# The closing tail of a two-layer encoder: a written-down order, split last columns, 1/rms by root and one Newton step

## The chip, the cores and the metric

The kernel runs on one core of one Trainium2 chip. The metric is the device time of one execution in microseconds, of which three were taken: 839.72, 839.94 and 842.06, median 839.94. One execution was recorded by the hardware profiler; its time is 839.72 and its span, from the first to the last instruction, 837.6. TensorE is called PE in the profile's rows, VectorE DVE, ScalarE ACT, GpSimd POOL, SyncE SP (it issues nearly all transfers).

## The reference

Two residual layers over 256 tokens of width 2048, each with a normalisation ahead, and a normalisation at the end. What matters here is the end:

```python
def rms_norm(x, g):
    xf = x.astype(jnp.float32)
    y = xf * lax.rsqrt(jnp.mean(xf * xf, axis=-1, keepdims=True) + EPS)
    return (y * g.astype(jnp.float32)).astype(x.dtype)
...
        if layer % 2 == 0:
            h = h + even_layer(y, w_in_even[i], w_out_even[i], rpb_b[i])
        else:
            h = h + odd_layer(y, w_in_odd[i], w_out_odd[i], sinks_c[i], qnorm_d[i], knorm_d[i])
    return rms_norm(h, final_g)
```

Each layer ends in an output projection, `mix @ w_out`, with a `mix` of 256 x 2048. All is float32 in and out.

## The kernel before

Tokens lie on the 128 partitions in two tiles, t = 0 and 1; the 2048 columns of the residual `h` are four blocks of 512, n = 0 to 3, `h[n][:, t, :]`. In the names of instructions these four are h_91 to h_94. Products in float32 are made of three matmuls (`mm3`, L100) out of operands split in two parts each, hence the three lines L102, L103, L104 in every product.

The output projection of the odd layer runs over eight head pairs. `close_layer` (L588) adds seven of them to `h` block by block; `ahead` loads the weights of the eighth into buffers of their own (named x in the rows) and the final weights `final_g`, spread over the partitions, into `gfin[n]`. `tail_odd` (L700) then does the last pair, and the final normalisation.

For each tile t, and each block n in it:

- `product_out` (L476): six matmuls of 512 columns into one of three buffers of PSUM (`ps_at`, L48). TensorE waits for a buffer until the addition three products earlier has read it.
- `add_h` (L495, VectorE): `h` += product.
- a Square on ScalarE (L722), which writes its result nowhere of use and gives the sum of squares of the block, `ss[n]`, by a read-out that is recorded as an instruction of its own.
- in the first tile, for the blocks 0 to 2, a multiplication of `h` by `gfin` (L724, VectorE).

After the third block the three sums so far are added (`head`, L728 and L729). After the fourth, `rsqrt_column` (L163) computes 1/rms for each row: an integer estimate and three Newton steps, nine instructions of one column on VectorE. `finish` (L704) scales a block by it and issues its output transfer: by one instruction that also multiplies by `gfin` (L707), or, for the blocks weighted already, on VectorE (L709) or ScalarE (L711).

The order of the instructions on each engine is decided by a scheduler that goes by priorities and takes the program's order among equals. Three things steer it here: `tc.high_priority(400)` moves the small operations on columns up, `tc.issue_after` puts one `finish` behind the last Square, and `tc.keep_in_program_order` (used by `pinned`, L85, for loads alone) keeps instructions in the order in which they are written. Every engine works its instructions off in order, and waits at the first one whose operands are not there.

Of the kernel before, what the change touches and what calls it, by code (L numbers as in the profile page):

```python
# [9 lines left out]
F32 = mybir.dt.float32  # L10
# [7 lines left out]
P = 128  # L18
# [16 lines left out]
def encoder(ctx, tc, a, out):  # L35
# [112 lines left out]
    def rsqrt(dst, ss, n, mean):  # L148
# [6 lines left out]
        for it in range(3):  # L155
# [5 lines left out]
            y = z  # L161

    def rsqrt_column(dst, ss, mean, rest):  # L163

        col = lambda name: sm.tile([P, 1], F32, tag="rc_" + name, name="rc_" + name)
        x = col("x")
        nc.vector.tensor_scalar(x, ss, mean, rest, ALU.mult, ALU.add)
        y = sm.tile([P, 1], I32, tag="rc_s", name="rc_s")
        nc.vector.tensor_scalar(y, x.bitcast(I32), -0.5, 1597463007.0, ALU.mult, ALU.add)
        y = y.bitcast(F32)  # L170
        half = col("half")
        nc.vector.tensor_scalar_mul(half, x, -0.5)
        for it in range(3):
            t = col("t")
            nc.vector.tensor_scalar(t, y, y, half, ALU.mult, ALU.mult)
            z = dst if it == 2 else col("z")
            nc.vector.tensor_scalar(z, t, 1.5, y, ALU.add, ALU.mult)
            y = z
# [521 lines left out]
    def tail_odd(order):  # L700

        scale = []

        def finish(n, t):  # L704
            y, r = h[n][:, t, :], scale[t]
            if t == 1 or n == NN - 1:
                nc.vector.scalar_tensor_tensor(y, y, r, gfin[n], ALU.mult, ALU.mult)  # L707
            elif n == 1:
                nc.vector.tensor_scalar_mul(y, y, r)  # L709
            else:  # L710
                nc.scalar.mul(y, y, r)  # L711
            nc.sync.dma_start(out[t * P : (t + 1) * P, n * 512 : (n + 1) * 512], y)

        for t in range(2):
            ss = [sm.tile([P, 1], F32, tag=f"fss{n}", name="fss") for n in range(NN)]
            head = None
            for n in range(NN):
                acc = ps_at.tile([P, 512], F32, tag="at", name="ps_t")
                product_out(acc, final[n], order[0], t, True, True)
                add_h(n, t, acc)  # L720
                junk = tp.tile([P, 512], BF16, tag="junk", name="junk", bufs=1)
                square = nc.scalar.activation(junk, h[n][:, t, :], AF.Square, accum_out=ss[n])  # L722
                if t == 0 and n < NN - 1:
                    nc.vector.tensor_mul(h[n][:, t, :], h[n][:, t, :], gfin[n])  # L724
# [102 lines left out]
```

## Time and profile before

| | |
|---|---|
| device time, three runs | 839.72, 839.94, 842.06 us |
| profiled execution: time, span | 839.72, 837.6 us |
| start of the tail's first matmul | 816.52 us |
| last matmul of the tail starts | 827.17 us |
| last instruction of VectorE starts, lasts | 833.68, 0.75 us |
| output transfers | 8 of 256 KB, issue to landing 2.1 us |
| products, additions, Squares in the tail | 8 x 6 matmuls, 8, 8 |

The page gives each engine's busy time and the chain of work that ended last: followed back from the last instruction, at each step to what released it, or to the instruction before it on its engine. A row of the timeline has the start in us from the span's start, the duration, engine, line, operation, what is written from what, and in brackets the idle time of the engine ahead of it with what ended it. A row of groups has the line, the count behind an x, the busy time in us, the mean duration in ns and the idle time ahead. Matmuls are pipelined: a row of 0.39 us is followed by the next after 0.23.

### The profile page before, as it was taken

How to read it: one execution, taken by the hardware profiler on the slowest of the kernel's cores; microseconds unless marked ns; L12 is line 12 of the kernel's file. 1: busy time of each engine (PE TensorE's matmuls, PEld its weight loads, DVE VectorE, ACT ScalarE, POOL GpSimd, SP SyncE). 2: the span in 40 equal slices, each digit the busy share in tenths (PEclk: the TensorE clock that was granted, in tenths of full speed). 3: DMA queues.
4: the chain of work that ended last, by engine and by line, in shares of the span. 5: the costliest groups of instructions: out<-in, count | busy, mean ns of one | idle time of the engine just before them, and what ended most of it. 6: DMA issues, size and time to landing. Idle time of an engine off the chain costs nothing.

```text
span 837.6 us, 11876 instructions
## 1 busy us (share of the span) xinstructions
PE 821.5 (98%) x4472; PEld 707.2 (84%) x4472; DVE 559.5 (67%) x873; ACT 445.1 (53%) x706; POOL 18.8 (2%) x24
## 2 busy tenths in 40 slices
PE   7999999999999999999999999999999999999995
PEld 5888888888888888888888888888899888888884
DVE  5677575667757675576645787786976666766547
ACT  6755454555445554455443565556666555664433
POOL 0000000000001010010000000000000000000000
PEclk9999999999999999999999999999999999999998
DMA  7976765655566565665555555654545555655622
GB/s 253 374 228 204 236 208 170 209 176 175 178 199 194 171 199 168 201 196 160 172 184 192 176 175 180 193 184 150 165 162 191 182 179 188 194 191 193 226 90 100
DMA packets 55577, 158.51 MB, mean 189 GB/s; under 512 B 14112, under 2 KB 15008, under 8 KB 55456
## 3 DMA queue, kind: packets, MB, share of 16 engines
q1 hardware_dynamic: 55376, 157.74, 57.7%
q8 instruction: 35, 0.57, 0.3%
q14 instruction: 22, 0.18, 0.1%
q10 hardware_dynamic: 144, 0.02, 0.0%
HBM read 155.64 MB, written 3.05 MB: 189 GB/s over the span
## 4 chain that ended last, share of the span: by engine, by line
PE 97%; DVE 1%; DMA 1%; ACT 0%; SPq 0%; issue 0%; DVEq 0%; ACTq 0%
PE ps_f L250 33%; PE ps_f L254 16%; PE ps_t L103 13%; PE ps_t L104 13%; PE ps_t L102 13%; PE ps_pt L439 2%; PE ps_s L103 1%; PE ps_s L104 1%; PE ps_out L103 1%; PE ps_out L104 1%; PE ps_s L102 1%; PE ps_out L102 1%; DMA wraw<-in_even_t 1%; PE ps_ht L610 0%; DVE h L495 0%; PE ps_tr L352 0%
## 5 line engine op out<-in xcount | busy, mean ns | idle before, releaser
L70 DVE TENSOR_TENSOR wlo<-wraw,whi 128x1024 fp32r<-128x1024 f32 (+1 forms) x269 | 329.5, 1225 | 209.7 <-ACT whi L69 208.6
L69 ACT CAST whi<-wraw 128x1024 fp32r<-128x1024 f32 (+1 forms) x269 | 281.8, 1048 | 345.5 <-PE ps_t L104 146.9
L250 PE MATMUL ps_f<-x,whi 128*128 128x512 f32 x1184 | 374.0, 397 | 0.0
L254 PEld LDWEIGHTS ps_f<-x,wlo 128*128 128x128 f32 x1184 | 222.3, 188 | 53.0 <-DVE wlo L70 0.7
L254 PE MATMUL ps_f<-x,wlo 128*128 128x256 f32 x1184 | 233.4, 278 | 0.0
L250 PEld LDWEIGHTS ps_f<-x,whi 128*128 128x128 f32 x1184 | 180.9, 189 | 0.4
L102 PE MATMUL ps_t<-whi,x 128*128 128x512 f32 (+1 forms) x256 | 97.7, 382 | 5.6 <-ACT x L95 5.6
L103 PE MATMUL ps_t<-wlo,x 128*128 128x512 f32 (+1 forms) x256 | 97.2, 380 | 0.3 <-DVE wlo L70 0.3
L104 PE MATMUL ps_t<-whi,x 128*128 128x512 f32 (+1 forms) x256 | 97.2, 380 | 0.0
L102 PE MATMUL ps_t<-whi,mh 128*128 128x512 f32 x240 | 94.1, 392 | 0.0
L103 PE MATMUL ps_t<-wlo,mh 128*128 128x512 f32 x240 | 94.0, 391 | 0.0
L104 PE MATMUL ps_t<-whi,ml 128*128 128x512 f32 x240 | 93.6, 390 | 0.0
L102 PEld LDWEIGHTS ps_t<-whi,x 128*128 128x128 f32 x256 | 48.4, 189 | 14.9 <-ACT x L95 6.8
L104 PEld LDWEIGHTS ps_t<-whi,x 128*128 128x128 f32 x256 | 48.4, 189 | 9.7 <-DVE x L96 0.6
L103 PEld LDWEIGHTS ps_t<-wlo,x 128*128 128x128 f32 x256 | 48.5, 189 | 9.2 <-DVE wlo L70 1.0
L104 PEld LDWEIGHTS ps_t<-whi,ml 128*128 128x128 f32 x240 | 45.1, 188 | 9.2
L103 PEld LDWEIGHTS ps_t<-wlo,mh 128*128 128x128 f32 x240 | 45.2, 188 | 8.9
L102 PEld LDWEIGHTS ps_t<-whi,mh 128*128 128x128 f32 x240 | 45.1, 188 | 8.9
L469 DVE TENSOR_TENSOR mx<-ps_out,silu 128x512 f32<-128x512 f32 x16 | 11.1, 691 | 30.1 <-PE ps_out L104 30.1
L495 DVE TENSOR_TENSOR h<-ps_t,h 128x512 f32<-128x512 f32 x32 | 21.1, 685 | 9.7 <-PE ps_t L104 9.5
L421 ACT ACTIVATE pr<-lg,mn 128x256 f32<-128x256 f32 (+1 forms) x48 | 23.9, 500 | 5.0 <-DVE mn L409 5.0
L294 DVE TENSOR_TENSOR qf<-ps_f,qf 128x512 f32<-128x512 f32 x37 | 25.2, 682 | 0.0
(116 smaller groups left out, 657.0 us busy)
## 6 DMA issues: line engine op xcount, KB each, us to landing
wraw<-in_even_f SPq DMA_DIRECT2D x96, 512.0 KB, 3.5
wraw<-in_odd_f SPq DMA_DIRECT2D x56, 512.0 KB, 3.4
wraw<-in_w_out_even SPq DMA_DIRECT2D x32, 512.0 KB, 3.3
wraw<-in_w_out_odd SPq DMA_DIRECT2D x32, 512.0 KB, 4.2
wraw<-in_even_t SPq DMA_DIRECT2D x31, 512.0 KB, 4.2
wraw<-in_odd_t SPq DMA_DIRECT2D x24, 512.0 KB, 3.6
h<-in_x SPq DMA_DIRECT2D x4, 512.0 KB, 8.0
bias<-in_bias_a SPq DMA_DIRECT2D x8, 256.0 KB, 5.2
```

The costliest lines, as they stand in the source:

```text
L69: nc.scalar.copy(self.hi[:, c], raw[:, c])
L70: nc.vector.tensor_sub(self.lo[:, c], raw[:, c], self.hi[:, c].bitcast(F32))
L102: nc.tensor.matmul(dst, lh, rh, start=first, stop=False, skip_group_check=True)
L103: nc.tensor.matmul(dst, lh, rl, start=False, stop=False, skip_group_check=True)
L104: nc.tensor.matmul(dst, ll, rh, start=False, stop=last, skip_group_check=True)
L250: nc.tensor.matmul(acc[:, f, :], w.hi[:, c], xx[k], start=k == 0, stop=False, skip_group_check=True)
L254: nc.tensor.matmul(acc[:, f, :S], w.lo[:, c], xh[k], start=False, stop=k == KC - 1, skip_group_check=True)
L294: nc.vector.tensor_add(f, acc[:, :, :S], f)
L421: nc.scalar.activation(p[:, t, :W], lg[:, t, :W], AF.Exp, bias=mn[:, t : t + 1], scale=-1.0, accum_out=den[:, t : t + 1],)
L439: nc.tensor.transpose(tr[:, c, t * P : (t + 1) * P], p[:, t, c * P : (c + 1) * P], ident)
L469: nc.vector.tensor_mul(m, o, silu)
L495: nc.vector.tensor_add(h[n][:, t, :], acc, h[n][:, t, :])
```

## The change

`tail_odd` is written anew; `rsqrt_column` goes, and `product_out` takes a slice of columns. All instructions of the tail on ScalarE, VectorE and SP, except the weightings, are kept in the order in which they are written. In the second tile the last block is done in two halves of 256 columns (product, addition, Square each apart, so five sums). 1/rms is now a square root on ScalarE (`rooted`), a reciprocal and one Newton step on VectorE (`scaled_row`). A first Sqrt is put behind the first Square, where the tables of ScalarE are switched. The weighting of a block stands right behind its own addition; block 0 of the second tile is weighted on GpSimd. The additions (1,1) to the last of the second tile stand around and ahead of the first tile's scalings, of which the one of block 3 comes almost last.

```diff
@@ product_out @@
-    def product_out(acc, c, pr, t, first, last):
+    def product_out(acc, c, pr, t, first, last, cols=slice(0, 512)):
         for hh in range(2):
-            k, n = slice(t * P, (t + 1) * P), slice(hh * 512, hh * 512 + 512)
+            k, n = slice(t * P, (t + 1) * P), slice(hh * 512 + cols.start, hh * 512 + cols.stop)
@@ tail_odd, rewritten @@
-        for t in range(2):
-            ss = [sm.tile([P, 1], F32, tag=f"fss{n}", name="fss") for n in range(NN)]
...
-        with tc.issue_after(square.ins):
-            finish(2, 0)
-        for n, t in ((1, 0), (3, 0), (0, 1), (1, 1), (2, 1), (3, 1)):
-            finish(n, t)
+        full, halves = slice(0, 512), [slice(0, 256), slice(256, 512)]
+        pin = tc.keep_in_program_order
+        cuts = [[(n, full) for n in range(NN)], [(n, full) for n in range(NN - 1)] + [(NN - 1, c) for c in halves]]
...
+        def added(t, i):
+            n, c = cuts[t][i]
+            width = c.stop - c.start
+            acc = ps_at.tile([P, 512], F32, tag="at", name="ps_t")[:, :width]
+            product_out(acc, final[n], order[0], t, True, True, c)
+            y = h[n][:, t, c]
+            pin(nc.vector.tensor_add(y, acc, y))
+            junk = tp.tile([P, 512], BF16, tag="junk", name="junk", bufs=1)[:, :width]
+            pin(nc.scalar.activation(junk, y, AF.Square, accum_out=ss[t][i]))
+
+        def weighted(n, t):
+            (nc.gpsimd if t else nc.vector).tensor_tensor(h[n][:, t, :], h[n][:, t, :], gfin[n], op=ALU.mult)
...
+        def rooted(t):
+            root = col("root")
+            pin(nc.scalar.activation(root, ss[t][-1], AF.Sqrt, bias=heads[t], scale=1.0 / D))
+            return root
+
+        def scaled_row(t, root):
+
+            y, x, half, u = [col(name) for name in ("y", "x", "half", "u")]
+            pin(nc.vector.tensor_scalar(x, ss[t][-1], 1.0 / D, heads[t], ALU.mult, ALU.add))
+            pin(nc.vector.tensor_scalar_mul(half, x, -0.5))
+            pin(nc.vector.reciprocal(y, root))
+            pin(nc.vector.tensor_scalar(u, y, y, half, ALU.mult, ALU.mult))
+            r = scale[t] = sm.tile([P, 1], F32, tag="fr", name="fr")
+            pin(nc.vector.tensor_scalar(r, u, 1.5, y, ALU.add, ALU.mult))
...
+        added(0, 0)
+        pin(nc.scalar.activation(warm, ss[0][0], AF.Sqrt))
+        weighted(0, 0)
+        added(0, 1)
+        weighted(1, 0)
+        added(0, 2)
+        weighted(2, 0)
+        first_sums(0)
+        added(0, 3)
+        root = rooted(0)
+        added(1, 0)
+        weighted(0, 1)
+        scaled_row(0, root)
+        finish(0, 0, "act")
+        added(1, 1)
+        finish(1, 0, "dve")
+        added(1, 2)
+        added(1, 3)
+        added(1, 4)
+        first_sums(1)
+        finish(2, 0, "dve")
+        another_sum(1)
+        scaled_row(1, rooted(1))
+        finish(3, 1, "both", halves[0])
+        finish(0, 1, "act")
+        finish(3, 1, "both", halves[1])
+        finish(3, 0, "both")
+        finish(2, 1, "both")
+        finish(1, 1, "both")
```

`first_sums` and `another_sum` add the sums of squares and scale them by 1/D; `finish` scales on ScalarE ("act"), on VectorE ("dve"), or on VectorE with the weights in the same instruction ("both").

The order that comes of it, at two places. First VectorE at the start of the tail, the first tile's four additions, before. L495 is the addition of a product, L724 the multiplication by the final weights, fhead the small sums.

```order
L495 TENSOR_TENSOR h_91<-ps_t,h_91 128x512
L495 TENSOR_TENSOR h_92<-ps_t,h_92 128x512
L724 TENSOR_TENSOR h_91<-h_91,gfin 128x512
L495 TENSOR_TENSOR h_93<-ps_t,h_93 128x512
L724 TENSOR_TENSOR h_92<-h_92,gfin 128x512
L495 TENSOR_TENSOR h_94<-ps_t,h_94 128x512
L728 TENSOR_SCALAR fhead<-fss 128x1
L724 TENSOR_TENSOR h_93<-h_93,gfin 128x512
L729 TENSOR_SCALAR fhead<-fhead 128x1
```

The same place in the changed kernel, whose line numbers differ: L697 is the addition, L702 the multiplication, L706 and L707 the sums.

```order
L697 TENSOR_TENSOR h_91<-ps_t,h_91 128x512
L702 TENSOR_TENSOR h_91<-h_91,gfin 128x512
L697 TENSOR_TENSOR h_92<-ps_t,h_92 128x512
L702 TENSOR_TENSOR h_92<-h_92,gfin 128x512
L697 TENSOR_TENSOR h_93<-ps_t,h_93 128x512
L702 TENSOR_TENSOR h_93<-h_93,gfin 128x512
L706 TENSOR_SCALAR fhead<-fss 128x1
L707 TENSOR_SCALAR fhead<-fhead 128x1
L697 TENSOR_TENSOR h_94<-ps_t,h_94 128x512
```

Each multiplication moved from behind the next block's addition to ahead of it, and the two sums from behind the fourth addition to ahead of it.

Then VectorE from the second tile's third product to the first scaling that follows its 1/rms (fr), before: h_93 and h_94 with ps_t are the additions, rc_ names the columns of `rsqrt_column`.

```order
L495 TENSOR_TENSOR h_93<-ps_t,h_93 128x512
L175 TENSOR_SCALAR rc_t<-rc_z,rc_half 128x1
L177 TENSOR_SCALAR fr<-rc_t,rc_z 128x1
L709 TENSOR_SCALAR h_92<-h_92,fr 128x512
L728 TENSOR_SCALAR fhead<-fss 128x1
L495 TENSOR_TENSOR h_94<-ps_t,h_94 128x512
L729 TENSOR_SCALAR fhead<-fhead 128x1
L707 SCALAR_TENSOR_TENSOR h_94<-h_94,fr,gfin 128x512
L167 TENSOR_SCALAR rc_x<-fss,fhead 128x1
L169 TENSOR_SCALAR rc_s<-rc_x 128x1
```

And in the changed kernel, from the scaling of the first tile's block 1 on; L738 scales on VectorE, L711 is the third sum, L724 to L729 are `scaled_row`.

```order
L738 TENSOR_SCALAR h_92<-h_92,fr 128x512
L697 TENSOR_TENSOR h_93<-ps_t,h_93 128x512
L697 TENSOR_TENSOR h_94<-ps_t,h_94 128x256 x2
L706 TENSOR_SCALAR fhead<-fss 128x1
L707 TENSOR_SCALAR fhead<-fhead 128x1
L738 TENSOR_SCALAR h_93<-h_93,fr 128x512
L711 TENSOR_SCALAR fhead<-fss,fhead 128x1
L724 TENSOR_SCALAR rc_x<-fss,fhead 128x1
L725 TENSOR_SCALAR rc_half<-rc_x 128x1
L726 RECIPROCAL rc_y<-rc_root 128x1
L727 TENSOR_SCALAR rc_u<-rc_y,rc_half 128x1
L729 TENSOR_SCALAR fr<-rc_u,rc_y 128x1
```

The additions of h_93 and h_94 now come behind the scaling of the first tile's h_92 and ahead of its h_93 (which ScalarE scaled before); the first tile's h_94, scaled ahead of the second 1/rms before, is scaled behind it.

More of the change, by code (lines that the diff above doesn't have):

```diff
@@ L160, in rsqrt @@
             nc.vector.scalar_tensor_tensor(z, t, 1.5, y, ALU.add, ALU.mult)
[L161 to L177, printed above, removed]
             y = z
@@ L700, in tail_odd @@
     def tail_odd(order):
[L702 to L709, printed above, removed]
-            else:
-                nc.scalar.mul(y, y, r)
-            nc.sync.dma_start(out[t * P : (t + 1) * P, n * 512 : (n + 1) * 512], y)
-        for t in range(2):
-            ss = [sm.tile([P, 1], F32, tag=f"fss{n}", name="fss") for n in range(NN)]
[L716 to L724, printed above, removed]
-                if n == NN - 2:
-                    head = sm.tile([P, 1], F32, tag="fhead", name="fhead")
-                    with tc.high_priority(400):
-                        nc.vector.tensor_scalar(head, ss[0], ss[1], ss[2], ALU.add, ALU.add)
-                        nc.vector.tensor_scalar(head, head, 1.0 / D, EPS, ALU.mult, ALU.add)
-            r = sm.tile([P, 1], F32, tag="fr", name="fr")
-            with tc.high_priority(400):
-                rsqrt_column(r, ss[-1], 1.0 / D, head)
-            scale.append(r)
-            if t == 0:
-                finish(0, 0)
@@ L736, in tail_odd @@
-        with tc.issue_after(square.ins):
-            finish(2, 0)
-        for n, t in ((1, 0), (3, 0), (0, 1), (1, 1), (2, 1), (3, 1)):
-            finish(n, t)
+        full, halves = slice(0, 512), [slice(0, 256), slice(256, 512)]
+        pin = tc.keep_in_program_order
+        cuts = [[(n, full) for n in range(NN)], [(n, full) for n in range(NN - 1)] + [(NN - 1, c) for c in halves]]
+        ss = [[sm.tile([P, 1], F32, tag=f"fss{t}{i}", name="fss", bufs=1) for i in range(4 + t)] for t in range(2)]
@@ new lines, in tail_odd @@
+        heads, scale = [None, None], [None, None]
+        def added(t, i):
[7 more added lines that the diff above has]
+            pin(nc.scalar.activation(junk, y, AF.Square, accum_out=ss[t][i]))
@@ new lines, in tail_odd @@
+        col = lambda name: sm.tile([P, 1], F32, tag="rc_" + name, name="rc_" + name)
+        def rooted(t):
[10 more added lines that the diff above has]
+            pin(nc.vector.tensor_scalar(r, u, 1.5, y, ALU.add, ALU.mult))
@@ new lines, in finish @@
+        def finish(n, t, how, cols=full):
+            y, r = h[n][:, t, cols], scale[t]
+            if how == "both":
+                pin(nc.vector.scalar_tensor_tensor(y, y, r, gfin[n][:, cols], ALU.mult, ALU.mult))
+            elif how == "act":
+                pin(nc.scalar.mul(y, y, r))
+            else:
+                pin(nc.vector.tensor_scalar_mul(y, y, r))
+            pin(nc.sync.dma_start(out[t * P : (t + 1) * P, n * 512 + cols.start : n * 512 + cols.stop], y))
+        added(0, 0)
```

8 lines of the change are left out of this document (added).

## The prediction

> **What bounds the kernel now.** I read the page first: the busy times and the chain of work that ended last.
>
> ```profile
> PE 821.5 (98%) x4472; PEld 707.2 (84%) x4472; DVE 559.5 (67%) x873; ACT 445.1 (53%) x706; POOL 18.8 (2%) x24
> PE 97%; DVE 1%; DMA 1%; ACT 0%; SPq 0%; issue 0%; DVEq 0%; ACTq 0%
> ```
>
> TensorE sets the time of 97% of the span, and the change touches nothing of that part: up to the closing tail the instructions stand in the same order on every engine. Only the last 20 us can move, so I read these by the instruction, engine by engine. First the chain in order of time, where it leaves TensorE:
>
> ```profile
> 821.89 0.24 PE ps_t L104
> 822.14 0.02 issue
> 822.16 0.69 DVE h L495
> ```
>
> From 822.16 on VectorE carries the chain (one Square on ScalarE excepted), although TensorE works until 827.56. So the tail is VectorE's queue, and its order is what counts. Now the timeline of the tail: start, duration, engine, line.
>
> ```profile
> 816.52 0.39 PE L102 MATMUL ps_t<-x,mh 128*128 128x512 f32 x1
> 824.68 0.39 PE L102 MATMUL ps_t<-x,mh 128*128 128x512 f32 x1
> 827.17 0.39 PE L104 MATMUL ps_t<-x,ml 128*128 128x512 f32 x1
> 816.72 2.05 DVE L495 TENSOR_TENSOR h<-ps_t,h 128x512 f32<-128x512 f32 x3 [5.85 <-PE ps_t L104]
> 819.44 0.69 DVE L495 TENSOR_TENSOR h<-ps_t,h 128x512 f32<-128x512 f32 x1 [0.67 <-PE ps_t L104]
> 820.05 0.68 DVE L724 TENSOR_TENSOR h<-h,gfin 128x512 f32<-128x512 f32 x1
> 827.99 0.68 DVE L495 TENSOR_TENSOR h<-ps_t,h 128x512 f32<-128x512 f32 x1
> 829.52 0.21 DVE L167 TENSOR_SCALAR rc_x<-fss,fhead 128x1 f32<-128x1 f32 x1
> 829.77 0.16 DVE L169 TENSOR_SCALAR rc_s<-rc_x 128x1 int32<-128x1 int32 x1
> 831.44 0.21 DVE L177 TENSOR_SCALAR fr<-rc_t,rc_z 128x1 f32<-128x1 f32 x1
> 833.68 0.75 DVE L707 SCALAR_TENSOR_TENSOR h<-h,fr,gfin 128x512 f32<-128x512 f32 x1
> 834.46 0.33 SPq L712 DMA_DIRECT2D out<-h  x1
> 818.80 0.63 ACT L722 ACTIVATE junk<-h 128x512 bf16<-128x512 f32 x1 [9.20 <-DVE h L495]
> 819.34 0.19 ACT L722 ACTIVATION_READ_ACCUMULATOR junk<-h 128x1 f32 x1
> 820.22 0.63 ACT L722 ACTIVATE junk<-h 128x512 bf16<-128x512 f32 x1 [0.70 <-DVE h L495]
> 829.30 0.19 ACT L722 ACTIVATION_READ_ACCUMULATOR junk<-h 128x1 f32 x1
> ```
>
> The eight products of the tail start 816.52 + 1.36 i (i = 0 to 7; i = 6 is the second row). The first addition is the last of the x3 group: 816.72 + 2.05 - 0.69 = 818.08 to 818.77. Four steps that I need again: an independent VectorE instruction starts 0.08 before the end of the one ahead (820.05 against 819.44 + 0.69); a dependent one 0.03 after it (829.77 against 829.52 + 0.21 = 829.73); VectorE to ScalarE takes 0.09 (820.13 to 820.22); ScalarE to VectorE 0.03 to 0.05 (829.49 to 829.52), taken as 0.04. A Square with its read-out is over 0.73 after it starts (819.34 + 0.19 - 818.80).
>
> The base for the sum is the profiled execution, 839.72: the last VectorE instruction ends at 833.68 + 0.75 = 834.43, and 5.29 us follow (output transfer, end of the span, what lies around the span). The median of the three runs is 0.22 higher, the highest 842.06.
>
> **Part 1: the weighting behind each addition.** Before, VectorE adds block n+1 and only then multiplies block n by its weights (820.05, after the addition of 819.44), so the Square that reads block n runs beside it. Now the multiplication stands right behind its own addition and writes what the Square still reads: VectorE waits for ScalarE three times, with the next addition queued behind it. One round is 0.69 addition + 0.09 + 0.73 Square + 0.04 + 0.60 for the multiplication = 2.15 us, against 1.36 of a product. So the first four additions start at 818.08, 820.23, 822.38 and, with the two small sums ahead of the last (0.27 by the L728 row in part 3, 0.03 and 0.06, so 0.36 more), 824.88; the fourth ends at 825.57. In the chain above it ended at 822.85. **Term 1: +2.72.** ACT's release may come at the end of the ACTIVATE instead of the read-out; that is 0.10 less for each round, so 2.4 to 2.7.
>
> TensorE feels this too: three buffers hold the products, so product 6 must wait for that fourth addition, and starts near 825.67, not 824.68. It is ready at 827.2, and VectorE comes to it only at 829.1 (below), so this pause is covered by VectorE's own lateness.
>
> **Part 2: the table switch on ScalarE.** It stands between the first and the second Square.
>
> ```profile
> 1.15 1.28 ACT L117 ACT_TABLE_LOAD   x1 [1.15 <-PEq L817]
> 2.44 0.20 ACT L117 ACTIVATE warm<-warm 128x1 f32<-128x1 f32 x1
> ```
>
> By the only load in this trace it takes 1.28, and the next ACTIVATE starts at once: 819.53 + 1.28 + 0.20 = 821.0. The second Square is due then anyway (820.91 + 0.09), so I cost the switch at nothing, but its cover is used up: anything more delays VectorE one for one, since its multiplication waits for that Square. The Trainium skill says otherwise: in "ScalarE: Activation LUTs", section What ACT_TABLE_LOAD costs, a switch is a load of about 1283 ns and a drain of about 1380 ns. The row agrees with the load and shows no drain; by the page the sum below would grow by about 1.4.
>
> **Part 3: the second tile, up to its last addition.** From 825.57 on: the addition (0,1) ends at 826.18; ScalarE squares from 825.66, reads out by 826.39, and takes the root.
>
> ```profile
> L426 DVE RECIPROCAL rden<-den 128x2 f32<-128x2 f32 x32 | 5.1, 158 | 0.2
> L709 DVE TENSOR_SCALAR h<-h,fr 128x512 f32<-128x512 f32 x1 | 0.5, 488 | 0.0
> L728 DVE TENSOR_SCALAR fhead<-fss 128x1 f32<-128x1 f32 x2 | 0.5, 266 | 0.0
> L339 DVE TENSOR_TENSOR ru<-rq,cosT 128x256 f32<-128x256 f32 x10 | 4.2, 417 | 0.0
> L96 DVE SCALAR_TENSOR_TENSOR x<-ps_ht,gcol,x 128x256 fp32r<-128x256 f32 x16 | 7.2, 478 | 0.8 <-ACT x L95 0.6
> L325 ACT ACTIVATE junk<-rq 128x128 bf16<-128x128 f32 x20 | 6.2, 310 | 0.1
> L175 DVE TENSOR_SCALAR rc_t<-rc_z,rc_half 128x1 f32<-128x1 f32 x4 | 1.1, 271 | 0.1
> L102 PE MATMUL ps_t<-whi,x 128*128 128x256 f32 x32 | 9.1, 286 | 0.0
> ```
>
> No Sqrt of a column is in the trace. Its bounds are the 0.20 of the warm-up and the 0.31 of a 128-column Square; I take 0.30, as it has a pointer operand like no warm-up has. So the root is there at 826.72; reciprocal (0.16), one Newton step (0.27 and 0.21) and three gaps give 827.46. Then the addition (1,1) until 828.07 and the scaling of block 1, 0.49 by its row. But GpSimd, idle in this tail before, now multiplies block 0 of the second tile from 827.44 (the read-out of its Square, queued behind the root). What VectorE does beside a 512-column multiplication of GpSimd, the trace shows:
>
> ```profile
> 299.60 1.22 DVE L70 TENSOR_TENSOR wlo<-wraw,whi 128x1024 fp32r<-128x1024 f32 x1
> 299.75 2.23 POOL L383 TENSOR_TENSOR bias<-maskB,rpb 128x512 f32<-128x512 f32 x1 [26.43 <-DVE silu L314]
> 300.93 1.46 DVE L431 TENSOR_SCALAR pr<-pr,rden 128x256 f32<-128x256 f32 x2
> 306.48 1.28 POOL L383 TENSOR_TENSOR bias<-maskB,rpb 128x512 f32<-128x512 f32 x1 [4.50 <-DMA rpb<-rows]
> 272.09 0.68 DVE L294 TENSOR_TENSOR qf<-ps_f,qf 128x512 f32<-128x512 f32 x1
> 271.00 2.32 POOL L383 TENSOR_TENSOR bias<-maskB,rpb 128x512 f32<-128x512 f32 x1 [7.38 <-DMA rpb<-rows]
> L431 DVE TENSOR_SCALAR pr<-pr,rden x32: 341/351/1199, 71.2 to 400.2; 128x256 f32<-128x256 f32 x32
> ```
>
> The two scalings took 1.46 together where one usually takes 0.35, and the second ended only 0.41 after GpSimd's end (299.75 + 2.23 = 301.98): the first was held until GpSimd was done. GpSimd in turn took 2.23 or 2.32 when it began beside a running VectorE subtraction, 1.28 when not. An addition out of PSUM (272.09) was not held. So here the addition (1,1) passes, GpSimd takes 1.28 (to 828.72), and the scaling of block 1 ends at 829.15 instead of 828.47: a hold of 0.68. With GpSimd at 2.32 it would be 1.7. The nearest row is 1.28, as only additions out of PSUM run beside its start.
>
> Behind the scaling are queued the addition (2,1), which ends at 829.76, and the halves of block 3, 0.42 each by a 256-column row (0.35 would be half of a 512-column addition and is the lower end): 830.10 and 830.44. Their products, twelve of 256 columns, are over at 829.05 by the pitch of 0.12 that such matmuls have (rows 618.29 and 618.41, below), also when the second half waits for the addition (1,1) to give back its buffer. From 825.57 to 830.44 are 4.87; before, from 822.85 to 828.67 (827.99 + 0.68), 5.82. **Term 2: -0.95**, the hold of 0.68 included.
>
> ```profile
> 618.29 0.28 PE L102 MATMUL ps_t<-whi,x 128*128 128x256 f32 x1
> 618.41 0.28 PE L103 MATMUL ps_t<-wlo,x 128*128 128x256 f32 x1
> ```
>
> **Part 4: last addition to 1/rms.** ScalarE is late as well: Square (2,1) starts at 829.85, the halves at 830.49 and 830.91 (0.42 each, between 0.31 for 128 columns and 0.63 for 512), and the last read-out ends at 831.43. VectorE's two sums wait for the first of these read-outs, and its scaling of block 2 and the third sum are over at 831.59. The root ends at 831.98, the Newton step at 832.73. That is 2.29 after the last addition, against 831.65 - 828.67 = 2.98. **Term 3: -0.69**, and -0.9 with a root of 0.20, since it is on the path twice.
>
> **Part 5: the last scalings.** Two halves of 0.48 and three whole blocks of 0.75, each 0.08 over the next: 832.76 to 835.64, 2.91 after the 1/rms; before, four blocks, 834.43 - 831.65 = 2.78. **Term 4: +0.13.** The block scaled by ScalarE is done at 833.5 and holds no transfer back; SP's nine issues of 0.33 find the queue free, and the last transfer is 256 KB as before.
>
> **Sum:** 2.72 - 0.95 - 0.69 + 0.13 = +1.21: the last scaling ends at 835.64, and with 5.29 behind it the profiled time is 840.9, 0.14% more. The bounds above (release, root, half widths) take off up to 0.6 and a GpSimd multiplication of 2.32 adds 1.0, so 840.3 to 841.9 is this case's own range. A measurement of this kernel can tell about 0.3%, 2.5 us, from no change, so I forecast no change that can be told.
>
> **Rivals.**
>
> A, the switch costs more than its load: nothing covers it. If ScalarE needs as long again as the load, 1.28, for the change of tables, the second Square starts at 822.3, and the whole queue behind it moves: 840.9 + 1.3 = 842.2, slower by 0.3%. It decides from the first tenth of a microsecond on. Against it stands the row at 2.44; for it, that at 1.15 ScalarE had nothing in flight to empty. By the page's figure, 842.3. A GpSimd multiplication of 2.32 on top of it would make 843.2. Chance 0.15.
>
> B, the waits of part 1 cost nothing: if the Square no longer held back the multiplication, additions would follow the products, the fourth ending at 823.4; the second tile's Newton step would end at 830.6 and the last scaling at 833.5, 0.9 earlier than before: 838.8, faster but within 0.3%. For it: the shorter Newton chain is real, 2.29 against 2.98. Against it: the multiplication writes in place over the block the Square reads, and its wait on ScalarE stands in the program. Chance 0.12.
>
> C, GpSimd does not hold the scaling (it starts later, or VectorE reaches it first): 0.7 less, 840.2. Against it the rows at 300.93. Chance 0.18.
>
> **How the numbers follow.** My forecast has 0.55, A 0.15, B 0.12, C 0.18. The predicted time is 840.9. The range goes from B's 838.8 to 842.4, A's 842.2 with the 0.2 by which the median stands over the profiled run. Faster by over 0.3% (below 837.4) needs more than B gives: 0.02. Slower by over 0.3% is the upper half of A: 0.08. Within: 0.90.
>
> **What would show it.** Right: in the new profile the first three additions on VectorE are 2.1 to 2.2 us apart, each multiplication released by ScalarE; TensorE pauses about 1 us ahead of product 6; the scaling of block 1 in the first tile takes over 1 us beside GpSimd's multiplication; the last scaling ends 1.2 us later. Wrong: a gap between the table load's end and the next ACTIVATE (A), multiplications that start 0.6 us after their additions (B), a scaling of 0.49 (C).

## The result and the profile after

| | before | after |
|---|---|---|
| median of 12 runs | 839.83 us | 841.30 us |
| lowest to highest | 838.75 to 842.06 | 840.33 to 843.73 |
| profiled execution: time, span | 839.72, 837.6 us | 840.33, 838.5 us |

The ratio of after to before is 1.0023, with a 95% interval of 1.0015 to 1.0031: the changed kernel is slower by 1.9 us (1.3 to 2.6; the medians differ by 1.47). That lies within the 0.3% that the prediction called no change, and the median is 0.4 us over its 840.9 and inside its range.

First the page of the changed kernel: busy times, and the chain that ended last by engine.

```profile
PE 822.5 (98%) x4478; PEld 708.9 (85%) x4478; DVE 558.5 (67%) x868; ACT 447.7 (53%) x712; POOL 19.4 (2%) x25
PE 94%; DMA 2%; DVE 2%; ACT 1%; SPq 0%; issue 0%; DVEq 0%; ACTq 0%
```

TensorE has six matmuls more (two halves for one block), VectorE five instructions fewer, GpSimd one more. The share of ScalarE in the chain grew from under 0.5% to 1%. The timeline of the tail shows why, VectorE first, then ScalarE, GpSimd and TensorE: start, duration, line, and in brackets the idle time ahead with what ended it.

```profile
817.12 0.69 DVE L697 TENSOR_TENSOR h<-ps_t,h 128x512 f32<-128x512 f32 x1
818.60 0.69 DVE L702 TENSOR_TENSOR h<-h,gfin 128x512 f32<-128x512 f32 x1 [0.79 <-ACT junk L699]
819.21 0.68 DVE L697 TENSOR_TENSOR h<-ps_t,h 128x512 f32<-128x512 f32 x1
820.73 0.69 DVE L702 TENSOR_TENSOR h<-h,gfin 128x512 f32<-128x512 f32 x1 [0.84 <-ACT junk L699]
821.34 0.68 DVE L697 TENSOR_TENSOR h<-ps_t,h 128x512 f32<-128x512 f32 x1
822.87 0.69 DVE L702 TENSOR_TENSOR h<-h,gfin 128x512 f32<-128x512 f32 x1 [0.85 <-ACT junk L699]
823.85 1.28 DVE L697 TENSOR_TENSOR h<-ps_t,h 128x512 f32<-128x512 f32 x2
826.95 0.99 DVE L738 TENSOR_SCALAR h<-h,fr 128x512 f32<-128x512 f32 x1
827.86 1.34 DVE L697 TENSOR_TENSOR h<-ps_t,h 128x512 f32<-128x512 f32 x3
830.16 0.21 DVE L711 TENSOR_SCALAR fhead<-fss,fhead 128x1 f32<-128x1 f32 x1
831.31 0.21 DVE L729 TENSOR_SCALAR fr<-rc_u,rc_y 128x1 f32<-128x1 f32 x1
831.56 2.87 DVE L734 SCALAR_TENSOR_TENSOR h<-h,fr,gfin 128x256 f32<-128x256 f32 x5
818.38 0.19 ACT L699 ACTIVATION_READ_ACCUMULATOR junk<-h 128x1 f32 x1
818.58 1.28 ACT L742 ACT_TABLE_LOAD   x1
819.88 0.20 ACT L742 ACTIVATE warm<-fss 128x1 f32<-128x1 f32 x1
819.99 0.62 ACT L699 ACTIVATE junk<-h 128x512 bf16<-128x512 f32 x1
830.25 0.19 ACT L699 ACTIVATION_READ_ACCUMULATOR junk<-h 128x1 f32 x1
830.47 0.29 ACT L718 ACTIVATE rc_root<-fss,fhead 128x1 f32<-128x1 f32 x1
826.37 1.29 POOL L702 TENSOR_TENSOR h<-h,gfin 128x512 f32<-128x512 f32 x1 [107.55 <-ACT junk L699]
824.59 0.50 PE L102 MATMUL ps_t<-x,mh 128*128 128x512 f32 x1 [0.71 <-DVE h L697]
```

Three multiplications by the weights (L702) each wait 0.8 us for ScalarE's Square (L699), and the first three additions stand 2.1 us apart, with products ready every 1.36. The chain of waits, in order of time, goes to and fro between the two engines:

```profile
820.08 0.62 ACT junk L699 x2
820.73 0.69 DVE h L702
821.42 0.61 DVE h L697
822.11 0.73 ACT junk L699 x2
822.87 0.69 DVE h L702
```

Square, multiplication, addition, Square: each waits for the one ahead, which is what a round of 2.1 us is made of. Behind the table load (818.58 + 1.28) the next ACTIVATE starts within 0.02. TensorE pauses 0.71 us ahead of the seventh product, until the fourth addition has given its buffer back. VectorE's last scaling ends at 831.56 + 2.87 = 834.43, by accident the same instant as before.

That instant misleads, because the tail began earlier in this execution. Its first matmul started at 815.56, not 816.52; between executions of all the kernels below that start lies anywhere from 815.56 to 819.46, although what precedes it is all but unchanged. So from here on I measure from the tail's own first matmul. The table has the profiled execution of every kernel; "1/rms" is the second tile's, "blocks" the output transfers, counted in blocks of 256 KB, that are issued behind it, and the last column is the whole tail up to the end of the execution. That end is the execution's time laid on the span's axis, so all that lies around the span is counted there. Each row is one execution.

| kernel | first matmul | to 1/rms | 1/rms to last scaling | last scaling to end of execution | 1/rms to end of execution | blocks | first matmul to end |
|---|---|---|---|---|---|---|---|
| before | 816.52 | 15.13 | 2.78 | 5.29 | 8.07 | 4 | 23.20 |
| after | 815.56 | 15.96 | 2.91 | 5.90 | 8.81 | 5 | 24.77 |
| weights later | 815.89 | 14.03 | 2.91 | 5.89 | 8.80 | 5 | 22.83 |
| no GpSimd | 816.59 | 15.45 | 2.91 | 5.89 | 8.80 | 5 | 24.25 |
| one transfer less | 816.71 | 15.97 | 2.91 | 5.30 | 8.21 | 4 | 24.18 |
| load early | 815.97 | 15.99 | 2.90 | 5.88 | 8.78 | 5 | 24.77 |
| four at the end | 818.15 | 14.15 | 2.25 | 5.88 | 8.13 | 4 | 22.28 |
| no GpSimd, four | 816.17 | 13.79 | 2.91 | 5.42 | 8.33 | 4 | 22.12 |
| before, transfer late | 816.43 | 15.14 | 2.77 | 6.00 | 8.77 | 5 | 23.91 |
| before, root alone | 815.73 | 13.75 | 2.78 | 5.32 | 8.10 | 4 | 21.85 |
| before, GpSimd column late | 819.46 | 15.13 | 2.78 | 5.46 | 8.24 | 4 | 23.37 |
| before, GpSimd column early | 816.40 | 15.13 | 2.78 | 5.45 | 8.23 | 4 | 23.36 |
| before, GpSimd block late | 817.17 | 15.13 | 2.78 | 5.38 | 8.16 | 4 | 23.29 |
| before, GpSimd block early | 816.10 | 15.13 | 2.77 | 5.41 | 8.18 | 4 | 23.31 |

From before to after the tail grew by 24.77 - 23.20 = 1.57 us, which the interval of the ratio holds: 0.83 up to the second 1/rms, 0.13 in the scalings, and 0.61 behind the last scaling. The prediction had foreseen the first two and put nothing in the third.

What happens there is read from a table by stretches: the stretch and its length, then busy time and count of instructions for each engine, the granted clock, the share of the DMA engines and what they moved in GB/s. Before, with stretches cut at the 1/rms, the first transfer's data and the last transfer's data:

```profile
831.65:833.30 1.65, 0.00 (x0) 0.00 (x0) 1.61 (x4) 0.00 (x0) 0.00 (x0) 0.50 0.02 6
833.30:836.10 2.80, 0.00 (x0) 0.00 (x0) 1.13 (x2) 0.00 (x0) 0.00 (x0) 0.50 0.99 374
836.10:837.60 1.50, 0.00 (x0) 0.00 (x0) 0.00 (x0) 0.00 (x0) 0.00 (x0) 0.50 0.01 1
```

The same of the changed kernel:

```profile
831.52:833.10 1.58, 0.00 (x0) 0.00 (x0) 1.54 (x5) 0.72 (x1) 0.00 (x0) 0.50 0.30 108
833.10:836.55 3.45, 0.00 (x0) 0.00 (x0) 1.32 (x2) 0.00 (x0) 0.00 (x0) 0.50 0.99 362
836.55:838.50 1.95, 0.00 (x0) 0.00 (x0) 0.00 (x0) 0.00 (x0) 0.00 (x0) 0.50 0.01 1
```

In the middle stretch all 16 DMA engines are busy (0.99). There the end is no longer VectorE's: the blocks queue for the DMA engines, four of them for 2.80 us before (0.70 each). Now five have to pass, and although the first half leaves earlier (0.30 of the first stretch), the queue is empty only 2.12 us after the last scaling (836.55 - 834.43), against 1.67 before. The last stretch has grown as well, from 1.50 to 1.95. Of this more below, since it turns out to be no cost.

### The profile page after: what moved, and what is told of

The parts are those of the page before. It is cut to its first block, busy times and chain, and to the rows that moved or that the text cites. A ratio compares the mean times of both kernels' runs of the same rounds, so it can differ in the third digit from the quotient of the medians.

```text
span 838.5 us, 11893 instructions
## 1 busy us (share of the span) xinstructions
PE 822.5 (98%) x4478; PEld 708.9 (85%) x4478; DVE 558.5 (67%) x868; ACT 447.7 (53%) x712; POOL 19.4 (2%) x25
## 4 chain that ended last, share of the span: by engine, by line
PE 94%; DMA 2%; DVE 2%; ACT 1%; SPq 0%; issue 0%; DVEq 0%; ACTq 0%
PE ps_f L233 33%; PE ps_f L237 16%; PE ps_t L102 12%; PE ps_t L103 12%; PE ps_t L104 12%; PE ps_pt L422 2%; DMA wraw<-in_even_t 1%; PE ps_s L103 1%; PE ps_s L104 1%; PE ps_out L103 1%; PE ps_out L104 1%; PE ps_s L102 1%; PE ps_out L102 1%; DMA h<-in_x 1%; ACT junk L699 0%; PE ps_ht L593 0%
## 5 line engine op out<-in xcount | busy, mean ns | idle before, releaser
L276 ACT COPY qf<-ps_f 128x512 f32<-128x512 f32 x37 | 21.4, 579 | 1.7 <-PE ps_f L237 1.7
```

Source lines behind the costliest of these rows:

```text
L276: nc.scalar.copy(f, acc[:, :, S:])
```

## The experiments

My theory after the result: the three waits for the Square cost some 2 us and are the change's only large price; the new 1/rms and the order of the second tile pay back a part; the rest is behind the last scaling. Rivals: the table load sets the rounds; GpSimd's multiplication costs more than it takes off VectorE; at the end it is the transfers, or else GpSimd.

### The weighting later

The weighting of a block moves behind the next block's addition, as it was in the kernel before; all else stays as changed.

```diff
         added(0, 0)
         pin(nc.scalar.activation(warm, ss[0][0], AF.Sqrt))
-        weighted(0, 0)
         added(0, 1)
-        weighted(1, 0)
+        weighted(0, 0)
         added(0, 2)
+        weighted(1, 0)
+        added(0, 3)
         weighted(2, 0)
         first_sums(0)
-        added(0, 3)
         root = rooted(0)
```

> The changed kernel with one thing undone: each weighting of the first tile stands again behind the next block's addition. If the three waits of VectorE for the Squares are what part 1 says, the fourth addition ends 6.6 us after the start of the tail's first matmul (9.0 in the changed kernel, 6.3 before), TensorE pauses no more ahead of product 6, and the last scaling ends 17.2 us after that start (18.9 and 17.9); the wait at the second weighting stays for 0.3 us because the table load delays the second Square. The time should fall by 1.7 us from the changed kernel's 841.3, to 839.6. Rival, the lateness comes from the POOL hold and the waits are covered: the last scaling stays at 18.9 and the time at 841.3.

838.72 us (838.04 to 840.47), 0.9993 of before (0.9984 to 1.0002). VectorE's timeline, then two rows of ScalarE:

```profile
818.82 0.69 DVE L697 TENSOR_TENSOR h<-ps_t,h 128x512 f32<-128x512 f32 x1 [0.67 <-PE ps_t L104]
821.07 0.69 DVE L702 TENSOR_TENSOR h<-h,gfin 128x512 f32<-128x512 f32 x1 [0.20 <-ACT junk L699]
821.67 0.68 DVE L697 TENSOR_TENSOR h<-ps_t,h 128x512 f32<-128x512 f32 x1
818.92 1.28 ACT L742 ACT_TABLE_LOAD   x1
820.33 0.61 ACT L699 ACTIVATE junk<-h 128x512 bf16<-128x512 f32 x1
```

Additions wait for products again; of the three waits for ScalarE one of 0.20 is left. It is the table load's, which the long rounds had hidden: the second Square starts at 820.33, behind the load and its Sqrt, although its addition ended at 818.82 + 0.69 = 819.51. In the version below that loads the table ahead of the tail and has the same order here (no GpSimd, four blocks) this multiplication waits for nothing. The fourth addition ends at 822.35, 6.46 us after the tail's first matmul (after: 8.98, before: 6.33), and the tail is 1.94 us shorter than that of the changed kernel. One edit, which moves no work to another engine, takes the loss away: the kernel can no longer be told from the one before. The last scaling ends 16.94 us after the tail's first matmul, 0.3 earlier than expected.

### No multiplication on GpSimd, and the table load ahead of the tail

Two versions of the changed kernel with one part altered, each measured in a single execution. The first leaves out the weighting of the second tile's block 0, so that block misses its final weights.

```diff
         added(1, 0)
-        weighted(0, 1)
         scaled_row(0, root)
```

> The changed kernel without the weighting on GpSimd; block 0 of the second tile is left without its final weights, so part of the output differs. If GpSimd holds VectorE's scaling of block 1, that scaling takes 0.49 us instead of 0.99 and what follows on VectorE comes 0.5 us earlier: last scaling 18.4 us after the tail's first matmul. Rival, the scaling is long for another reason (its operand): it stays at 0.99.

The row that was 0.99 beside GpSimd:

```profile
827.99 0.48 DVE L738 TENSOR_SCALAR h<-h,fr 128x512 f32<-128x512 f32 x1
```

840.84 us, with a tail 0.52 us shorter than that of the changed kernel (24.25 against 24.77). The hold costs 0.99 - 0.48 = 0.51 and is on the path in full. The second version loads the table ahead of the tail's first product.

```diff
+        pin(nc.scalar.activation(warm, warm, AF.Sqrt))
         added(0, 0)
-        pin(nc.scalar.activation(warm, ss[0][0], AF.Sqrt))
         weighted(0, 0)
```

> The changed kernel with the first Sqrt, and so the table load, ahead of the tail's first Square, in ScalarE's idle time. By part 2 the load is just covered where it stands: the second Square starts 4.43 us after the tail's first matmul in the changed kernel; without the load it would start 0.0 to 0.1 us earlier, so the last scaling stays at 18.9 and the last transfers at 4.1 us behind it. Rival, the switch costs more than its load: the second Square comes earlier by more than 0.3 us.

840.74 us. Here the second Square waits for its addition:

```profile
820.40 0.63 ACT L699 ACTIVATE junk<-h 128x512 bf16<-128x512 f32 x1 [1.42 <-DVE h L697]
```

It starts 820.40 - 815.97 = 4.43 us after the tail's first matmul, and with the load in the tail at 819.99 - 815.56 = 4.43 as well. The tail is the same 24.77. The load was covered to the hundredth, with nothing to spare and nothing lost. The Trainium skill, in "ScalarE: Activation LUTs", section What ACT_TABLE_LOAD costs, adds a drain of about 1380 ns to a load of about 1283 ns; the load agrees with the 1.28 here, and no run here shows the drain.

### The transfers at the end

The first of these leaves out the transfer of the first tile's block 3, so these columns of the output are not written.

```diff
-            pin(nc.sync.dma_start(out[t * P : (t + 1) * P, n * 512 + cols.start : n * 512 + cols.stop], y))
+            if (n, t) != (3, 0):
+                pin(nc.sync.dma_start(out[t * P : (t + 1) * P, n * 512 + cols.start : n * 512 + cols.stop], y))
```

> The changed kernel without the output transfer of the first tile's block 3, which is left unwritten; all engines work as before. From the last scaling's end to the end of the span there were 3.17 us before and 4.07 in the changed kernel. Theory: the sixteen DMA engines are busy without a break from the first transfer behind the second 1/rms, with five blocks of 256 KB instead of four at some 380 GB/s, so one block less takes 0.69 us off: 3.4 us. Rival, the end is a fixed latency behind the last issue that varies from execution to execution: 4.07 stays, or any value from 3.2 to 4.1 comes without the DMA share of 1.0 until the end.

840.89 us in one execution, from a tail that began 1.15 us later. From the last scaling to the end of the execution 5.30 us, where the changed kernel has 5.90 and the kernel before 5.29. The opposite test takes the kernel before, moves no work of any engine, and only issues that block's transfer behind the second tile's first one.

```diff
-            nc.sync.dma_start(out[t * P : (t + 1) * P, n * 512 : (n + 1) * 512], y)
+            late = tc.keep_in_program_order if t else lambda x: x
+            if (n, t) != (3, 0):
+                late(nc.sync.dma_start(out[t * P : (t + 1) * P, n * 512 : (n + 1) * 512], y))
+            if (n, t) == (0, 1):
+                late(nc.sync.dma_start(out[:P, 1536:], h[3][:, 0, :]))
```

> The kernel of before with nothing moved but one output transfer: that of the first tile's block 3 is issued behind the first of the second tile's, so that five blocks of 256 KB are sent behind the second 1/rms as in the changed kernel. All engines work as before: last scaling 17.9 us after the tail's first matmul. Theory: the sixteen DMA engines are the end of the kernel, so the end comes 0.7 us later (3.9 us behind the last scaling instead of 3.17), and the time rises by 0.7. Rival, the end hangs on the last transfer alone, which is issued when it was: 3.17 stays and the time is the same.

839.78 us, 1.0004 of before (0.9995 to 1.0013), so the time alone decides nothing. The tail does: up to the last scaling it is the kernel before to the hundredth (17.91 us), then 6.00 us follow instead of 5.29. The table by stretches shows the queue:

```profile
833.20:836.65 3.45, 0.00 (x0) 0.00 (x0) 1.14 (x2) 0.00 (x0) 0.00 (x0) 0.50 1.01 378
836.65:838.20 1.55, 0.00 (x0) 0.00 (x0) 0.00 (x0) 0.00 (x0) 0.00 (x0) 0.50 0.02 5
```

3.45 us at a full share for five blocks (0.69 each), the length that the changed kernel has. One block more behind the 1/rms costs 0.6 to 0.7 us, and one less gives it back: the count of blocks alone separates 8.07 to 8.33 from 8.77 to 8.81 in the column from 1/rms to end, over all fourteen kernels. The number of transfers does not: the first version of the next section issues nine like the changed kernel, four blocks of them behind the 1/rms, and has 8.13.

### Four blocks at the end, two versions

With the weightings later and the load early, the first tile's block 3 is scaled and sent ahead of the second 1/rms. The first version keeps GpSimd.

```diff
         added(1, 1)
-        finish(1, 0, "dve")
         added(1, 2)
+        finish(1, 0, "dve")
+        finish(2, 0, "dve")
         added(1, 3)
...
-        finish(2, 0, "dve")
         another_sum(1)
-        scaled_row(1, rooted(1))
+        root = rooted(1)
+        finish(3, 0, "both")
+        scaled_row(1, root)
...
-        finish(3, 0, "both")
         finish(2, 1, "both")
```

> All parts of the change kept, with three places altered: weightings behind the next addition, the table load ahead of the first Square, and the first tile's four blocks all scaled and sent ahead of the second 1/rms (block 3 while VectorE waits for the root; block 1 behind the addition (2,1), out of GpSimd's way). The last scaling should end 15.9 us after the tail's first matmul (16.9 in the run with the weightings alone put back, 17.9 before) and, with four blocks of output behind the second 1/rms instead of five, the span should end 3.2 to 3.5 us behind it (4.07 with five): a time of 837.2, 0.3% below the kernel of before. Rival, that the end behind the last scaling does not go by the number of blocks: 4.0 stays, and the time is 838.

838.88 us, 0.9989 of before (0.9980 to 0.9998); one of its twelve executions took 4705.39 us, for which the record has no reason, and is left out of the ratio. The 837.2 expected is missed, and the last scaling ends 16.40 us after the tail's first matmul, not 15.9. From the last scaling to the end of the span are 4.05 us, where 3.2 to 3.5 was expected: a third miss, and its reason lies in what I counted from. With only 2.25 us of scalings behind the 1/rms VectorE is done earlier than the DMA queue; the queue begins at the 1/rms, and from there to the end of the execution it is 8.13, as with every kernel of four blocks. The second version takes GpSimd away too, and scales block 0 of the second tile on VectorE in place of ScalarE.

```diff
-        weighted(0, 1)
...
         added(1, 1)
-        finish(1, 0, "dve")
+        finish(3, 0, "both")
         added(1, 2)
+        finish(1, 0, "dve")
...
         finish(3, 1, "both", halves[0])
-        finish(0, 1, "act")
         finish(3, 1, "both", halves[1])
-        finish(3, 0, "both")
         finish(2, 1, "both")
         finish(1, 1, "both")
+        finish(0, 1, "both")
```

> Like the run with four blocks at the end, but GpSimd and ScalarE take no part in the second tile's scaling: block 0 is scaled and weighted by VectorE as the last. No hold by GpSimd is then possible, and the first tile's block 3 is scaled right behind the addition (1,1). The 1/rms should come as early as there or 0.2 earlier; the last scaling, one block more on VectorE, ends 16.4 us after the tail's first matmul, and the span 3.2 to 3.5 us behind it, as one transfer follows another at the pace of the scalings: 837.6. If the DMA engines and not VectorE set the pace of the end, it comes out within 0.4 of the run with four blocks at the end.

838.30 us, 0.9986 (0.9977 to 0.9995). The tail is 22.12 us, 1.08 below that of the kernel before; the last scaling ends 16.70 us after the tail's first matmul, where 16.4 was expected, and the time is 0.7 over the 837.6 expected.

### The root alone

The kernel before, with nothing of the new order, only 1/rms by a root and one Newton step, and the table load behind the first Square.

```diff
@@ rsqrt_column @@
-        y = sm.tile([P, 1], I32, tag="rc_s", name="rc_s")
-        nc.vector.tensor_scalar(y, x.bitcast(I32), -0.5, 1597463007.0, ALU.mult, ALU.add)
...
+        roots.append(nc.scalar.activation(root, ss, AF.Sqrt, bias=rest, scale=mean))
...
+        nc.vector.reciprocal(y, root)
+        nc.vector.tensor_scalar(u, y, y, half, ALU.mult, ALU.mult)
+        nc.vector.tensor_scalar(dst, u, 1.5, y, ALU.add, ALU.mult)
@@ tail_odd @@
+                if t == 0 and n == 0:
+                    tc.keep_in_program_order(square)
+                    tc.keep_in_program_order(nc.scalar.activation(warm, ss[0], AF.Sqrt))
...
-        with tc.issue_after(square.ins):
+        with tc.issue_after(roots[-1].ins):
             finish(2, 0)
```

> The kernel of before with one part of the change alone: 1/rms by a root on ScalarE, a reciprocal and one Newton step, with the table load behind the first Square; whole blocks, the scheduler's order, the weightings behind the next addition, no GpSimd. ScalarE's scaling of block 2 of the first tile stands behind the second root, so that it does not hold it back. If term 3 stands for the gain in the change and terms 1 and 2 and the fifth block at the end for the loss, the second 1/rms is done 2.1 to 2.3 us after the last addition (2.98 before), the last scaling ends 16.4 to 17.2 us after the tail's first matmul (17.9 before), and the span 6.2 us behind the second 1/rms as with four blocks at the end: 838.4 to 839.2. Rival, the root brings nothing since ScalarE's queue is in its way: 17.9 and the time of before.

837.95 us, 0.9980 of before (0.9971 to 0.9989): the lowest median here, though its interval overlaps those of the two versions with four blocks. It beats the kernel before by 1.7 us and the changed one by more, and is faster than the 838.4 to 839.2 expected. The rows of VectorE that carry it:

```profile
826.90 0.69 DVE L492 TENSOR_TENSOR h<-ps_t,h 128x512 f32<-128x512 f32 x1
828.44 0.21 DVE L169 TENSOR_SCALAR rc_x<-fss,fhead 128x1 f32<-128x1 f32 x1 [0.48 <-ACT junk L719]
829.27 0.21 DVE L175 TENSOR_SCALAR fr<-rc_u,rc_y 128x1 f32<-128x1 f32 x1
829.52 2.74 DVE L704 SCALAR_TENSOR_TENSOR h<-h,fr,gfin 128x512 f32<-128x512 f32 x4
```

From the end of the last addition (827.59) to the second 1/rms (829.48) it takes 1.89 us, where the kernel before needs 2.98 and the changed one 2.32 (2.1 to 2.3 was expected). In the changed kernel the root starts 830.47 - 829.20 = 1.27 after the last addition, here 0.85 after it (the sum at 828.44 waits for the same read-out as the root): with the additions in a row, ScalarE has the Square of block 2 and those of both halves to do one behind the other. The version with halves and a scaling ahead of them (no GpSimd, four blocks) takes 2.03. No run takes the halves alone out of the changed kernel, so their own price isn't shown; none of these figures speaks for them.

### GpSimd in the tail

The last stretch of the span, behind the last data, was 1.50 to 1.60 us without GpSimd in the tail and 1.80 to 1.95 with it. To see whether a GpSimd instruction is the reason, the kernel before gets one that nothing reads: first a copy of one column, in the tail or early in the program.

```diff
+                if t == 0 and n == 0:
+                    nc.gpsimd.tensor_copy(warm, ss[0])
                 if t == 0 and n < NN - 1:
```

> The kernel of before with one instruction of a single column put on GpSimd in the tail, behind the first Square; nothing reads it. In the five runs with GpSimd's weighting in the tail the span ends 0.7 us after SP's last drain, in the five without 0.3 us. If an instruction of GpSimd so late is the cause, this run ends 0.6 to 0.8 us after SP's last drain, with the last scaling 17.9 us after the tail's first matmul as before. If it is the other edits of the tail, it ends 0.3 us after it.

```diff
         nc.gpsimd.tensor_scalar_mul(nsink, sink, -1.0)
+        nc.gpsimd.tensor_copy(warm, sink[:, :1])
```

> The same single-column instruction, but 100 us after the start, where GpSimd has other work. If what counts is that GpSimd works late, the span ends 0.3 us after SP's last drain as before; if what counts is the number of its instructions, 0.6 to 0.8 us.

842.83 and 839.76 us, one execution each. The first began its tail 3 us late: in its first 100 us the granted clock was 0.98 where the other has 1.00, and nothing of this lies in the tail. From the last scaling to the end of the span they have 3.23 and 3.19. A copy of one column does nothing there, so that form of the theory fell. Then with the changed kernel's own instruction, a multiplication of 128x512 into a spare tile, behind the second tile's second addition or behind the first tile's first.

```diff
+                if (t, n) == (1, 1):
+                    extra = tp.tile([P, 2, S], F32, tag="tmp", name="extra", bufs=4)
+                    nc.gpsimd.tensor_mul(extra.rearrange("p c t -> p (c t)"), h[n][:, t, :], gfin[n])
                 if t == 0 and n < NN - 1:
```

> The kernel before, with one GpSimd multiplication of 128x512 f32 (as the changed kernel has one, 1.3 us) into a spare tile that nothing reads, behind the second tile's second addition; no other work and no transfer is moved, and four blocks of 256 KB stay behind the second 1/rms. The earlier look with a copy of one column at 822.5 us did not lengthen the end (837.37 to 840.6 = 3.2 us behind the last scaling, the kernel before 3.17). Theory that a GpSimd instruction of this size in the tail makes the closing sequence longer: last scaling to end of the span 3.5 to 3.7 us, and from the last drain of SP's queue to the end about 0.7 us. Rival, that the longer closing in the changed kernel comes from something else in it: 3.1 to 3.25 us and about 0.4.

The other has `(0, 0)` in place of `(1, 1)`.

> As the run beside it, with the same GpSimd multiplication behind the first tile's first addition, some 6 us earlier in the tail. If the size of the instruction alone lengthens the closing sequence: last scaling to end 3.5 to 3.7 us here as well. If its lateness does: 3.1 to 3.25 us here and 3.5 to 3.7 in the other. If neither: 3.1 to 3.25 us in both. The shares of the DVE path ahead may shift by up to 0.7 us, since the multiplication can hold a DVE instruction that lies beside it; they are not what is read here.

840.46 and 839.41 us, one execution each. The late one's last stretch, behind the last data:

```profile
836.70:838.60 1.90, 0.00 (x0) 0.00 (x0) 0.00 (x0) 0.00 (x0) 0.00 (x0) 0.50 0.02 5
```

The early one's last stretch:

```profile
835.65:837.50 1.85, 0.00 (x0) 0.00 (x0) 0.00 (x0) 0.00 (x0) 0.00 (x0) 0.50 0.01 3
```

The closing drains of SP's queue (count, durations in ns, first and last start) in the late one, whose span ends at 838.6:

```profile
L826 SPq DRAIN  x3: 7/7/7, 837.5 to 837.8; - x3
```

And in the kernel before, whose span ends at 837.6, so 0.4 behind the last drain, not 0.8:

```profile
L823 SPq DRAIN  x3: 7/7/7, 836.9 to 837.2; - x3
```

So a multiplication of this size on GpSimd, at either place in the tail, does lengthen the end of the span, by 0.3 to 0.4 us (3.52 and 3.50 behind the last scaling instead of 3.17). But it lengthens only the span. What lies around the span is shorter by nearly as much: 840.46 - 838.6 = 1.86 and 839.41 - 837.5 = 1.91, where the kernel before has 839.72 - 837.6 = 2.12. All kernels with this multiplication in the tail have 1.82 to 1.91 there, all without it 2.12 to 2.26. In the execution's own time 5.38 and 5.41 us follow the last scaling, 0.1 more than the 5.29 before and less than the 5.45 of the early column copy. What GpSimd does at its end so that the span's limit moves stays open; whether the size or the kind of instruction decides it was not tried. In the execution's time no cost of it can be told.

## Why the prediction came out as it did

By its steps, each against the tail's first matmul so that the later start of other executions stays out.

- **Part 1, the weighting behind each addition: right.** Foreseen +2.72, from rounds of 2.15 us; measured rounds of 2.09, 2.13 and 2.51 (the last with the two sums), and a fourth addition that ends 8.98 us after the first matmul, not 6.33: +2.65. The experiment with the weightings later takes it away. Rival B is out. TensorE's pause came as described (the seventh product 0.87 late, 0.71 of it idle) and was covered as described: no later addition waits for a product.
- **Part 2, the table switch: right, and as tight as it said.** It fills the round exactly; rival A, which needed a loss from the first tenth of a microsecond, is out by the early load. In kernels without the long rounds the load does show, as the 0.20 in the experiment with later weightings; the kernel with the root alone has the same 0.20 there.
- **Part 3, the second tile: right, a size off.** Foreseen -0.95, measured from 824.54 to 829.20 = 4.66 against 5.82: -1.16. The hold by GpSimd, 0.68 in the sum, was 0.51, since the scaling ended 0.28 after GpSimd's multiplication (827.94 against 827.66), not 0.43 as I had taken; the halves took less than 0.42 each, 1.34 for three additions. GpSimd's price of 1.28 came true (1.29), but the row it was taken from had been misread: the multiplication at 306.48 did begin beside a running subtraction, in its last 0.13 us (305.38 + 1.23 = 306.61). Rival C is out: the scaling was held, though its 0.99 stayed just under the "over 1 us" named as a sign.
- **Part 4, last addition to 1/rms: the number right, the path not.** Foreseen 2.29, measured 831.52 - 829.20 = 2.32, with a root of 0.29 to 0.30. The prediction let the root wait for VectorE's third sum, with the last read-out 0.16 us earlier. In the trace that sum is over at 830.16 + 0.21 = 830.37, the read-out only at 830.25 + 0.19 = 830.44, and the root starts 0.03 behind it. The read-out ended 1.24 us after the last addition, not 0.99: the last three Squares start at 828.63, 829.39 and 829.93, so 0.76 and 0.54 apart, the later two each 0.03 behind the read-out of the one ahead, where the sum had 0.64 and 0.42. That the total came out is in part luck: the root ended 0.32 behind what released it (830.76 against 830.44), where the sum had 0.39.
- **Part 5, the last scalings: right.** 2.91 foreseen and measured.
- **Behind the last scaling: wrong, and the largest error of the sum.** The prediction let 5.29 us follow the last scaling as before, because "SP's nine issues of 0.33 find the queue free, and the last transfer is 256 KB as before". Both halves of that sentence consider single transfers, and neither the queue of the DMA engines. These are full from the first whole block behind the 1/rms, and the change sends five blocks there instead of four. The term measured 5.90: +0.61. Of this, 0.45 is the later end of the last data (1.67 to 2.12 us behind the last scaling). The remaining 0.16 is what the longer end of the span (+0.45) leaves after the shorter time around it (-0.29); the kernel before with one late transfer, which has no GpSimd in the tail, has +0.71 in all, so I do not put those 0.16 down to GpSimd.

The sum: up to the last scaling +0.96 where +1.21 was foreseen, and behind it +0.61 where nothing was, together +1.57 for +1.21. The profiled execution shows only +0.61 (840.33 against 839.72), because its tail began 0.96 us earlier. The 12 runs put the loss at 1.9 us (1.3 to 2.6), which holds the 1.57; the 1.21 lies just below. So the 840.9 owes some of its nearness to luck: 0.25 too much up to the last scaling hides part of the 0.61 that was left out. And the forecast of no change that can be told took too coarse a measure: twelve executions of each kernel tell 0.08% either way, a quarter of the 0.3% it allowed, and they do tell this change.

## What to carry to other kernels

An in-place write belongs behind the next independent instruction of its engine, not right behind the instruction whose result another engine is still reading: three waits of 0.8 us cost 1.94 us here, with every queue in a fixed order. At the end of a kernel, count the bytes that can leave only after the last scalar is known, not the length of the last transfer: each block of 256 KB there was 0.6 to 0.7 us of the profiled tail, whoever scaled it. And a rewrite with several ideas is worth taking apart: the root with one Newton step alone gives 0.9980 of the time, and the rest of the change turned that into 1.0023.

## What the hardware showed besides

- At the end of the program all 16 DMA engines were busy at 362 to 378 GB/s in the kernel before (four blocks), the changed kernel and the one with a late transfer (five each). In the three versions that send four blocks with the halves among them the share was 0.92 to 0.96, with 333 to 348 GB/s. The issue of the late transfer took SP 0.43 us and the three behind it 0.39 to 0.42, where the eight issues of the kernel before took 0.33 to 0.35.
- A scaling of 128x512 on VectorE out of and into SBUF took 0.99 beside GpSimd's multiplication and 0.48 without it, and ended 0.28 behind it; the addition out of PSUM that started 0.02 ahead of that multiplication was not held (0.68).
- The span's end moved by 0.3 to 0.4 us with a GpSimd multiplication of 128x512 in the tail, and the time around the span by -0.2 to -0.3. A span is no substitute for the execution's time where few tenths are weighed.
